# Where the two halves of each split weight unit lie in on-chip memory, and a 64-byte offset for the units of q, k and w_glu

## The chip, the cores and the metric

The kernel runs on one core of a Trainium2 chip. The time is device microseconds of one execution, taken as the median of several runs. One further execution was profiled; the views and the rows below come from it.

## What is computed

One decoder layer (depth 1) of width 2048 over 256 tokens. Three branches work side by side on the normalised input, their outputs are gated and summed, and a squared-ReLU MLP follows:

```python
proj = xn @ w_in          # 2048 x 11264: u_s5, u_lru, q, k, v, three gates
y_s5 = s5_branch(...)     # diagonal scan, gelu, y * sigmoid(y @ w_glu)
y_lru = rglru_branch(...)
y_attn = stick_breaking_attention(q, k, v)
merged = g_s5 * (y_s5 @ w_br_s5) + g_lru * (y_lru @ w_br_lru) + g_attn * (y_attn @ w_br_attn)
h = x + merged @ w_out
h = h + relu(rms_norm(h) @ w_up) ** 2 @ w_down
out = rms_norm(h)
```

Everything is float32. Nearly all of the time goes to the weight products.

## The kernel before

**Units.** All weight matrices are cut into units of 256 rows by 512 columns (two row blocks of 128, `UK = 2`, and `CH = 512` columns); a unit fills 128 partitions with 2 x 512 floats, 512 KB. The list `stream` fixes their order. Each unit is loaded by one DMA from the SP queue into a tile `raw` (three buffers), and split in two: ScalarE (ACT) writes the rounded copy `hi` (line 146), VectorE (DVE) writes the remainder `lo = raw - hi` (line 147). Both are float32r. The activations are split the same way (`xhi`, `xlo` and their like). A product is then three TensorE matmuls: high by high, high by low, low by high.

**Two forms of product.** In `chunk` (lines 225 to 227) the unit is the stationary operand, 128 columns at a time, and the activations are the moving one, 256 tokens wide: 2 row blocks x 4 column tiles x 3 = 24 matmuls a unit. It serves the columns 0 to 7 of `w_in`, 512 wide each (0 and 1: input of the S5 branch; 2 and 3: of the LRU branch; 4 and 5: q; 6 and 7: k), and `w_glu`. In `chunk_tok` (lines 241 to 243) and `pair_tok` (lines 276 to 278) the unit is the moving operand, 512 columns wide, and 128 tokens of the activations are stationary: 2 x 2 x 3 = 12 matmuls a unit. They serve all other products. Each matmul instruction has a weight load of its own, which the profile shows apart as PEld.

**Order.** `next_unit` keeps loads four units and splits three units ahead of the unit in use. The pools `whi` hold four buffers for `hi` and four for `lo`, so the split of a unit needs the matmuls of the unit four places earlier to be done. Side work (norms, the S5 scan, the LRU and the attention) is written as generators, which `pump` advances after every unit. Line 655 belongs to the S5 scan: it takes the sums `ps_y` from PSUM, whose matmuls are at line 653. `s5_stack` (line 631) copies pieces of `ux` into `stk` by DMAs on the SP queue, the queue of the unit loads (line 130). Tile addresses follow the order in which pools and tiles are made, in steps of 32 bytes; a scheduler orders the instructions of each engine.

**Addresses.** A byte address here is that within a partition, and its residue is that modulo 256. In the program before, `hi`, `lo`, `xhi`, `xlo` and all operands of the three forms of product begin at residue 32. The four `hi` buffers lie 4096 bytes apart, the four `lo` buffers too, and each stands off the activations by a multiple of 4096 bytes. Inside a tile the slices move by multiples of 512 bytes.

Of the kernel before, what the change touches and what calls it, by code (L numbers as in the profile page):

```python
# [9 lines left out]
F32 = mybir.dt.float32  # L10
F32R = mybir.dt.float32r
# [3 lines left out]
P = 128  # L15
# [3 lines left out]
CH = 512  # L19
UK = 2  # L20
W = 1024
WT = W // P
# [16 lines left out]
GELU_K = 0.044715  # L39


def units_of(k, n):
    return (n // CH) * (k // (P * UK))

# [2 lines left out]
def hybrid_block(ctx: ExitStack, tc: tile.TileContext, io, out):  # L47
# [2 lines left out]

    const = ctx.enter_context(tc.tile_pool(name="const", bufs=1))
    wraw = ctx.enter_context(tc.tile_pool(name="wraw", bufs=3))
    whi = ctx.enter_context(tc.tile_pool(name="whi", bufs=4))
    act = ctx.enter_context(tc.tile_pool(name="act", bufs=1))
    ypool = ctx.enter_context(tc.tile_pool(name="ypool", bufs=2))
    tmp = ctx.enter_context(tc.tile_pool(name="tmp", bufs=2))
    psm = ctx.enter_context(tc.tile_pool(name="psm", bufs=4, space=PSUM))
    pss = ctx.enter_context(tc.tile_pool(name="pss", bufs=4, space=PSUM))
# [2 lines left out]
    stream = []  # L61
# [36 lines left out]
    for q in range(NQ):  # L98
# [5 lines left out]
        for c in range(2, 4):  # L104
            stream.extend(("w_down", c, q * (FQ // (P * UK)) + g) for g in range(FQ // (P * UK)))
    ngrp = {"w_in": D, "w_br_lru": W, "w_br_attn": W, "w_br_s5": W, "w_glu": W,
            "w_out": D, "w_up": D, "w_down": DFF}

    raw, hi, anchor = {}, {}, {}
    st = {"load": 0, "split": 0, "use": 0}  # L110

    def pieces(i):
        return [slice(k, k + 1) for k in range(UK)] if i == 0 else [slice(0, UK)]
# [19 lines left out]
    def split_next():  # L133
        i = st["split"]
        if i >= len(stream):
            return
        st["split"] += 1
        h = whi.tile([P, UK, CH], F32R, tag="hi", name=f"hi{i}")
        l_ = whi.tile([P, UK, CH], F32R, tag="lo", name=f"lo{i}")
        r = raw.pop(i)  # L140
        x = anchor.pop("x", None)
        es = ExitStack()
        if i == 0:
            es.enter_context(tc.issue_after(x))
        for k in pieces(i):
            anchor["act"] = nc.scalar.copy(h[:, k, :], r[:, k, :]).ins  # L146
            anchor["dve"] = nc.vector.tensor_tensor(l_[:, k, :], r[:, k, :], h[:, k, :].bitcast(F32), ALU.subtract).ins  # L147
        es.close()
        hi[i] = h, l_

    def next_unit():
        i = st["use"]
        st["use"] += 1
        while st["load"] <= min(i + 4, len(stream) - 1):
            load_next()
            load_x(st["load"])
        while st["split"] <= min(i + 3, len(stream) - 1):
            before_split(st["split"])
            split_next()
        return (stream[i], *hi.pop(i))  # L160
# [126 lines left out]
    def small(name):  # L287
        o = 0
        for n_, w_ in PAR.items():
            if n_ == name:  # L290
                return par[:, o:o + w_]
            o += w_
# [39 lines left out]
    nc.gpsimd.affine_select(keep, ones, pattern=[[1, P]], compare_op=ALU.is_gt, fill=0.0, base=0, channel_multiplier=-1)  # L332
    drop = const.tile([P, P], F32, name="drop")
    nc.gpsimd.tensor_scalar(drop, keep, 1e30, -1e30, ALU.mult, ALU.add)
    eps_t = const.tile([P, 1], F32, name="eps_t")
    nc.gpsimd.memset(eps_t, EPS)
    half_pi = const.tile([P, 1], F32, name="half_pi")
    nc.gpsimd.memset(half_pi, math.pi / 2)
    magic = const.tile([P, 1], F32, name="magic")
    nc.gpsimd.memset(magic, MAGIC)  # L340

    def rsqrt_mean(o, ps, n):
# [4 lines left out]
        nc.vector.scalar_tensor_tensor(o, t, 1.5, r, ALU.add, ALU.mult)  # L347

    rstd = const.tile([P, L], F32, name="rstd")
    rstd_tok = const.tile([P, 2], F32, name="rstd_tok")  # L350

    def norm1():
        yield
# [131 lines left out]
    br_ = small("lru_b_r")  # L485
    bi_ = small("lru_b_i")
    lam = small("lru_lambda")
    sp4 = const.tile([P, WT], F32, name="sp4")
    nsp8 = const.tile([P, WT], F32, name="nsp8")
    tiny = const.tile([P, 1], F32, name="tiny")  # L490
    nc.gpsimd.memset(tiny, 2.0 ** -115)
    wrwi = sp.tile([P, 2, WT, P], F32, tag="stk", name="wrwi")
    wr, wi = wrwi[:, 0], wrwi[:, 1]
# [3 lines left out]
    def lru_load():  # L497
        for t, src in ((wr, "lru_w_r"), (wi, "lru_w_i")):
            for h in range(2):
                nc.sync.dma_start(t[h * 64:(h + 1) * 64, :, h * 64:(h + 1) * 64], io[src][h])  # L500
                yield

    def lru_params():
        for _ in range(4):
            yield
        lc = const.tile([P, 4, WT], F32, name="lc")
        nc.vector.scalar_tensor_tensor(lc[:, 0, :], lam, -1.0, lam, ALU.mult, ALU.min)
        nc.scalar.activation(lc[:, 1, :], lc[:, 0, :], AF.Exp)
        nc.scalar.activation(lc[:, 2, :], lc[:, 1, :], AF.Ln, bias=1.0)
        nc.vector.tensor_scalar(lc[:, 3, :], lam, -1.0, 0.0, ALU.mult, ALU.max)  # L510
        nc.vector.tensor_tensor(lc[:, 3, :], lc[:, 3, :], lc[:, 2, :], ALU.add)
        nc.vector.tensor_scalar(sp4, lc[:, 3, :], 4.0, None, ALU.mult)
        nc.vector.tensor_scalar(nsp8, lc[:, 3, :], -8.0, None, ALU.mult)
        yield
        yield from lru_load()
# [4 lines left out]
    def lru_half(c, us):  # L520
# [44 lines left out]
        for u, cts, xc, r, i_, th in parts:  # L565
# [5 lines left out]
            yield  # L571

    lq = later([lru_params()], 1.15)
    u_banks = {}

# [315 lines left out]
    for c in range(2):  # L891
        banks = chunk("w_glu", c, W, lambda kt: (yg_hi[:, kt, :], yg_lo[:, kt, :]))
        for j in range(2):
            g = tmp.tile([P, 2, L], F32, tag="gate", name=f"glu_{c}_{j}", bufs=3)
            for h in range(2):
                k = c * 4 + 2 * j + h
# [24 lines left out]
    for a in S5_TAIL:  # L921
        c = int(a[1])
# [52 lines left out]
                yield  # L975
        return gen

    rs2 = const.tile([P, 2], F32, name="rs2")
    rq, rfl = [deque(), 2.0, 0.0], {}

    def out_done(c, banks):
# [199 lines left out]
```

## Time and profile before

| | us |
|---|---|
| median of 3 runs | 1490.29 |
| lowest and highest | 1489.69, 1490.58 |
| the profiled execution, its own time | 1491.41 |
| its span in the trace | 1489.7 |
| TensorE busy in the span | 1478.5 |
| VectorE busy | 1175.7 |
| ScalarE busy | 775.4 |

The page gives for each engine its busy time, its share of the span and its instructions. A matmul's duration in the page is longer than the distance to the next one, since matmuls overlap: how fast TensorE gets on is read from the starts of matmuls that follow each other in the timeline, not from the durations. PEld rows are the weight loads of the same matmuls, which run beside the matmul before.

### The profile page before, as it was taken

The page shows a single profiled execution, that of the slowest core. Times are in us where ns is not written, and L with a number is a line of the kernel's source. Part 1 is how long each engine was busy: PE and PEld are TensorE (multiplying, and loading weights), DVE is VectorE, ACT ScalarE, POOL GpSimd, SP SyncE. Part 2 cuts the span into 40 slices and gives each one's busy share as a digit, 9 for nine tenths or more (in the row PEclk, how much of TensorE's full clock was granted, in tenths as well). Part 3 has the DMA queues.
Part 4 walks back from the last instruction along what each step waited for, and adds up shares of the span by engine and source line. Part 5 has one row for each costly group of instructions (what it writes and reads, how often), then busy time and mean ns, then how long its engine had stood idle before and what let it go on. Part 6 is the DMA issues. An engine that isn't in the chain of part 4 may idle for free.

```text
span 1489.7 us, 19903 instructions
## 1 busy us (share of the span) xinstructions
PE 1478.5 (99%) x7518; PEld 1259.3 (85%) x7518; DVE 1175.7 (79%) x1470; ACT 775.4 (52%) x915; POOL 48.4 (3%) x73
## 2 busy tenths in 40 slices
PE   9999999999999999999999999999999999999997
PEld 9998888989888888888888888888888888888886
DVE  6878999887989998789799896568754886458955
ACT  6767556565765564544454544344433453344443
POOL 1400000000000000000000000000000000000010
PEclk9999999999999999999999999999999999999999
DMA  9557776655556756566856657666666566666664
GB/s 274 189 157 216 209 229 208 184 165 188 170 177 199 224 184 210 188 187 210 268 183 189 195 184 222 189 193 188 200 194 196 187 197 197 192 190 196 189 198 137
DMA packets 89570, 292.41 MB, mean 196 GB/s; under 512 B 12802, under 2 KB 17026, under 8 KB 89346
## 3 DMA queue, kind: packets, MB, share of 16 engines
q1 hardware_dynamic: 89042, 290.55, 62.5%
q8 instruction: 59, 0.97, 0.3%
q10 hardware_dynamic: 432, 0.59, 0.1%
q14 instruction: 37, 0.30, 0.1%
HBM read 282.71 MB, written 2.10 MB: 191 GB/s over the span
## 4 chain that ended last, share of the span: by engine, by line
PE 95%; DVE 2%; ACT 1%; DMA 1%; issue 1%; DVEq 0%; ACTq 0%; SPq 0%
PE mt_w_in L241 7%; PE mt_w_in L243 7%; PE mt_w_in L242 7%; PE mt_w_up L241 7%; PE mt_w_up L243 7%; PE mt_w_up L242 7%; PE mp_w_down L278 4%; PE mp_w_down L277 4%; PE mp_w_down L276 4%; PE mt_w_down L242 4%; PE mt_w_down L241 4%; PE mt_w_down L243 4%; PE mm_w_in L225 3%; PE mm_w_in L227 3%; PE mm_w_in L226 3%; PE mt_w_br_attn L241 1%
## 5 line engine op out<-in xcount | busy, mean ns | idle before, releaser
L146 ACT CAST hi<-raw 128x1024 fp32r<-128x1024 f32 (+1 forms) x521 | 545.2, 1050 | 614.2 <-PE mt_w_up L243 116.8
L147 DVE TENSOR_TENSOR lo<-raw,hi 128x1024 fp32r<-128x1024 f32 (+1 forms) x521 | 637.1, 1224 | 276.2 <-ACT hi L146 268.5
L241 PE MATMUL mt_w_in<-hi,xhi 128*128 128x512 f32 x448 | 176.2, 393 | 0.0
L243 PE MATMUL mt_w_in<-hi,xlo 128*128 128x512 f32 x448 | 174.5, 389 | 0.0
L242 PE MATMUL mt_w_in<-lo,xhi 128*128 128x512 f32 x448 | 174.4, 389 | 0.0
L241 PE MATMUL mt_w_up<-hi,hhi 128*128 128x512 f32 x448 | 174.3, 389 | 0.0
L242 PE MATMUL mt_w_up<-lo,hhi 128*128 128x512 f32 x448 | 174.3, 389 | 0.0
L243 PE MATMUL mt_w_up<-hi,hlo 128*128 128x512 f32 x448 | 174.3, 389 | 0.0
L225 PE MATMUL mm_w_in<-xhi,hi 128*128 128x256 f32 x512 | 146.7, 287 | 0.7 <-ACT hi L146 0.7
L227 PE MATMUL mm_w_in<-xhi,lo 128*128 128x256 f32 x512 | 145.6, 285 | 1.4 <-DVE lo L147 1.4
L226 PE MATMUL mm_w_in<-xlo,hi 128*128 128x256 f32 x512 | 145.6, 285 | 0.0
L741 DVE STREAM_TRANSPOSE reluT<-relu 32x256 f32<-32x256 f32 x256 | 111.5, 436 | 4.2
L242 PE MATMUL mt_w_down<-lo,hd_hi 128*128 128x512 f32 (+1 forms) x272 | 102.5, 377 | 0.0
L241 PE MATMUL mt_w_down<-hi,hd_hi 128*128 128x512 f32 (+1 forms) x272 | 102.4, 377 | 0.0
L243 PE MATMUL mt_w_down<-hi,hd_lo 128*128 128x512 f32 (+1 forms) x272 | 102.4, 376 | 0.0
L225 PEld LDWEIGHTS mm_w_in<-xhi,hi 128*128 128x128 f32 x512 | 99.1, 194 | 1.9 <-ACT hi L146 1.0
L227 PEld LDWEIGHTS mm_w_in<-xhi,lo 128*128 128x128 f32 x512 | 98.8, 193 | 1.9 <-DVE lo L147 1.8
L276 PE MATMUL mp_w_down<-hi,hd_hi 128*128 128x512 f32 x256 | 99.6, 389 | 0.0
L277 PE MATMUL mp_w_down<-lo,hd_hi 128*128 128x512 f32 x256 | 99.6, 389 | 0.0
L278 PE MATMUL mp_w_down<-hi,hd_lo 128*128 128x512 f32 x256 | 99.6, 389 | 0.0
L226 PEld LDWEIGHTS mm_w_in<-xlo,hi 128*128 128x128 f32 x512 | 99.2, 194 | 0.1
L243 PEld LDWEIGHTS mt_w_in<-hi,xlo 128*128 128x128 f32 x448 | 84.1, 188 | 17.7
(294 smaller groups left out, 2358.1 us busy)
## 6 DMA issues: line engine op xcount, KB each, us to landing
raw<-in_w_in SPq DMA_DIRECT2D x175, 512.0 KB, 4.2
raw<-in_w_up SPq DMA_DIRECT2D x128, 512.0 KB, 4.3
raw<-in_w_down SPq DMA_DIRECT2D x128, 512.0 KB, 4.2
raw<-in_w_out SPq DMA_DIRECT2D x32, 512.0 KB, 4.4
raw<-in_w_br_lru SPq DMA_DIRECT2D x16, 512.0 KB, 4.6
raw<-in_w_br_attn SPq DMA_DIRECT2D x16, 512.0 KB, 4.3
raw<-in_w_br_s SPq DMA_DIRECT2D x16, 512.0 KB, 4.3
stk<-ux SPq DMA_DIRECT2D x96, 64.0 KB, 4.3
```

The source lines that it names most:

```text
L146: anchor["act"] = nc.scalar.copy(h[:, k, :], r[:, k, :]).ins
L147: anchor["dve"] = nc.vector.tensor_tensor(l_[:, k, :], r[:, k, :], h[:, k, :].bitcast(F32), ALU.subtract).ins
L225: nc.tensor.matmul(o, wh[:, kk, s], xh, start=first and ct % 2 == 0, stop=False, skip_group_check=True)
L226: nc.tensor.matmul(o, wh[:, kk, s], xl, start=False, stop=False, skip_group_check=True)
L227: mm = nc.tensor.matmul(o, wl[:, kk, s], xh, start=False, stop=last and ct % 2 == 1, skip_group_check=True)
L241: nc.tensor.matmul(banks[j], xh[:, s], wh[:, a:b], start=kt == 0, stop=False)
L242: nc.tensor.matmul(banks[j], xh[:, s], wl[:, a:b], start=False, stop=False)
L243: return nc.tensor.matmul(banks[j], xl[:, s], wh[:, a:b], start=False, stop=kt == ng * UK - 1)
L276: nc.tensor.matmul(o, xh[:, s], wh[:, kk, :], start=kt == 0, stop=False)
L277: nc.tensor.matmul(o, xh[:, s], wl[:, kk, :], start=False, stop=False)
L278: mm = nc.tensor.matmul(o, xl[:, s], wh[:, kk, :], start=False, stop=kt == ng * UK - 1)
L741: nc.vector.transpose(d_[32 * a:32 * a + 32, :, :, 32 * b:32 * b + 32], s_[32 * b:32 * b + 32, :, :, 32 * a:32 * a + 32])
```

## The change

The pool `whi` goes. A new pool `wsplit` holds four slots with tags `w0` to `w3`, one for every fourth unit. A slot holds the high half, behind it the low half, and 16 floats (64 bytes) to spare. The function `shift` says where in the slot a unit begins: at the slot's start, or 16 floats (64 bytes) on for `w_glu` and for columns 4 to 7 of `w_in`. A slot takes 8256 bytes. Small tiles that lay in the pool `const` are put between the slots, with some filling (`row`), so that slots stand 8448 bytes apart, 33 times 256.

```diff
+SLOTS = 4
+SHIFT = 16
+
+
+def shift(name, c, g):
+    return SHIFT if name == "w_glu" or name == "w_in" and 4 <= c < 8 else 0
...
-    whi = ctx.enter_context(tc.tile_pool(name="whi", bufs=4))
     act = ctx.enter_context(tc.tile_pool(name="act", bufs=1))
     ypool = ctx.enter_context(tc.tile_pool(name="ypool", bufs=2))
+    wsplit = ctx.enter_context(tc.tile_pool(name="wsplit", bufs=1))
...
+    def slot(i):
+        return wsplit.tile([P, 2 * UK * CH + SHIFT], F32R, tag=f"w{i % SLOTS}", name=f"w{i % SLOTS}_{i}")
+
+    def row(name, n, used=None):
+        return wsplit.tile([P, n], F32, name=name)[:, 0:used or n]
+
+    first = [slot(0)]
+    lc, sp4, nsp8 = row("lc", 4 * WT).rearrange("p (a k) -> p a k", a=4), row("sp4", WT), row("nsp8", WT)
+    first.append(slot(1))
+    eps_t, half_pi, magic, tiny = (row(n, 1) for n in ("eps_t", "half_pi", "magic", "tiny"))
+    rstd_tok = row("rstd_tok", 16, 2)
+    first.append(slot(2))
+    rs2 = row("rs2", 48, 2)
+    first.append(slot(3))
...
-        h = whi.tile([P, UK, CH], F32R, tag="hi", name=f"hi{i}")
-        l_ = whi.tile([P, UK, CH], F32R, tag="lo", name=f"lo{i}")
+        o = shift(*stream[i])
+        w = (first[i] if i < SLOTS else slot(i))[:, o:o + 2 * UK * CH]
+        h, l_ = (w[:, a:a + UK * CH].rearrange("p (k c) -> p k c", k=UK) for a in (0, UK * CH))
```

The other lines of the diff take the tiles `eps_t`, `half_pi`, `magic`, `tiny`, `rstd_tok`, `sp4`, `nsp8`, `lc` and `rs2` out of the pool `const`.

In the program after, every operand of the three forms of product begins at residue 160, except the shifted units: their `hi` and `lo` begin at residue 224, 64 bytes on from the activations that they meet. Slots 0 and 2 stand off the activations by a multiple of 512 bytes, slots 1 and 3 by 256 bytes more.

TensorE has the same matmuls in the same order, with the same engines waited for. This is the start of the first q unit on TensorE, before, where `hi` and `lo` are two tiles:

```order
1588 L227 MATMUL mm_w_in_1_80_2536<-xhi,lo_2690 128x256
1589 L225 MATMUL mm_w_in_0_88_2825<-xhi,hi_2720 128x256 [waits Activation_49]
1590 L226 MATMUL mm_w_in_0_88_2825<-xlo,hi_2720 128x256
1591 L227 MATMUL mm_w_in_0_88_2825<-xhi,lo_2721 128x256 [waits DVE_49]
1592 L225 MATMUL mm_w_in_0_88_2825<-xhi,hi_2720 128x256
```

And the same place on TensorE after the change, where `w_88` is the slot of unit 88:

```order
1588 L251 MATMUL mm_w_in_1_80_2454<-xhi,w_87_2603 128x256
1589 L249 MATMUL mm_w_in_0_88_2735<-xhi,w_88_2633 128x256 [waits Activation_49]
1590 L250 MATMUL mm_w_in_0_88_2735<-xlo,w_88_2633 128x256
1591 L251 MATMUL mm_w_in_0_88_2735<-xhi,w_88_2633 128x256 [waits DVE_49]
1592 L249 MATMUL mm_w_in_0_88_2735<-xhi,w_88_2633 128x256
```

Nothing moved: the first high matmul waits for ScalarE alone, and the first low one for VectorE.

On VectorE the subtraction of a unit no longer waits for TensorE. Within the first k columns VectorE has, before, this order; `lo_2591` is the low half of unit 84:

```order
249 L147 TENSOR_TENSOR lo_2540<-raw_2500,hi_2539 128x1024 [waits DMAHW6_49,Activation_49]
250 L621 TENSOR_TENSOR ux<-us_99,ux 128x256 [waits Activation_49]
251 L625 SCALAR_TENSOR_TENSOR ux<-bco,par,ux 128x2x64 [waits Activation_49] x2
252 L147 TENSOR_TENSOR lo_2591<-raw_2537,hi_2590 128x1024 [waits DVE_49,DMAHW7_49,PE_49,Activation_49]
253 L655 SCALAR_TENSOR_TENSOR us_99<-us_99,par,ps_y_2578 128x256 [waits PE_49]
254 L679 TENSOR_TENSOR s_t<-s_v,tc_2110 128x1024 [waits DVE_49]
```

The same place on VectorE after the change:

```order
247 L171 TENSOR_TENSOR w_83_2457<-raw_2419,w_83_2457 128x1024 [waits DMAHW6_49,Activation_49]
248 L637 TENSOR_TENSOR ux<-us_112,ux 128x256 [waits Activation_49]
249 L641 SCALAR_TENSOR_TENSOR ux<-bco,par,ux 128x2x64 [waits Activation_49] x2
250 L671 SCALAR_TENSOR_TENSOR us_112<-us_112,par,ps_y_2495 128x256 [waits PE_49]
251 L171 TENSOR_TENSOR w_84_2507<-raw_2455,w_84_2507 128x1024 [waits DMAHW7_49,DVE_49,Activation_49]
252 L695 TENSOR_TENSOR s_t<-s_v,tc_2046 128x1024 [waits DVE_49]
```

The subtraction of unit 84 moved behind the instruction that takes `ps_y` out of PSUM (line 655 before, 671 after), which waits for TensorE. The same swap is made once more, at unit 122. The wait of a subtraction on TensorE went, since ScalarE, which writes the slot first, holds that wait for both halves. In a `chunk` unit ScalarE now waits for the last matmul of the unit four places earlier, where it waited for the last but one.

On the SP queue three unit loads change places with one small DMA of `s5_stack` each. Before, at the second such place:

```order
160 L631 DMA stk<-ux 32x512 [waits DMAHW1_49]
161 L130 DMA raw_2827<-in_w_in 128x1024 [waits DMAHW2_49,DVE_49]
162 L631 DMA stk<-ux 32x2x256 [waits DMAHW3_49]
163 L130 DMA raw_2861<-in_w_in 128x1024 [waits DMAHW5_49,DMAHW4_49,DVE_49]
```

The same place on the SP queue after the change:

```order
160 L647 DMA stk<-ux 32x512 [waits DMAHW1_49]
161 L647 DMA stk<-ux 32x2x256 [waits DMAHW2_49]
162 L153 DMA raw_2737<-in_w_in 128x1024 [waits DMAHW3_49,DVE_49]
163 L153 DMA raw_2770<-in_w_in 128x1024 [waits DMAHW5_49,DMAHW4_49,DVE_49]
```

One unit load moved one place back. On ScalarE and VectorE a few instructions of one LRU step change places too.

More of the change, by code (lines that the diff above doesn't have):

```diff
@@ L334, in hybrid_block @@
     nc.gpsimd.tensor_scalar(drop, keep, 1e30, -1e30, ALU.mult, ALU.add)
-    eps_t = const.tile([P, 1], F32, name="eps_t")
     nc.gpsimd.memset(eps_t, EPS)
-    half_pi = const.tile([P, 1], F32, name="half_pi")
     nc.gpsimd.memset(half_pi, math.pi / 2)
-    magic = const.tile([P, 1], F32, name="magic")
     nc.gpsimd.memset(magic, MAGIC)
@@ L349, in hybrid_block @@
     rstd = const.tile([P, L], F32, name="rstd")
-    rstd_tok = const.tile([P, 2], F32, name="rstd_tok")
     def norm1():
@@ L487, in hybrid_block @@
     lam = small("lru_lambda")
-    sp4 = const.tile([P, WT], F32, name="sp4")
-    nsp8 = const.tile([P, WT], F32, name="nsp8")
-    tiny = const.tile([P, 1], F32, name="tiny")
     nc.gpsimd.memset(tiny, 2.0 ** -115)
@@ L505, in lru_params @@
             yield
-        lc = const.tile([P, 4, WT], F32, name="lc")
         nc.vector.scalar_tensor_tensor(lc[:, 0, :], lam, -1.0, lam, ALU.mult, ALU.min)
@@ L976, in residual @@
         return gen
-    rs2 = const.tile([P, 2], F32, name="rs2")
     rq, rfl = [deque(), 2.0, 0.0], {}
```

## The prediction

> **What bounds the kernel now.** I read the page's shares first, then who waited for whom on TensorE, then the timeline of TensorE, because the page's matmul durations overlap and say nothing of the pace.
>
> ```profile
> span 1489.7 us, 19903 instructions
> PE 1478.5 (99%) x7518; PEld 1259.3 (85%) x7518; DVE 1175.7 (79%) x1470; ACT 775.4 (52%) x915; POOL 48.4 (3%) x73
> ...
> PEclk9999999999999999999999999999999999999999
> ...
> PE 95%; DVE 2%; ACT 1%; DMA 1%; issue 1%; DVEq 0%; ACTq 0%; SPq 0%
> ```
>
> TensorE is busy 99% of the span at the full granted clock, and 95% of the chain that ended last is its own. The waits on TensorE confirm it; these three rows are all there are:
>
> ```profile
> PE mm_w_in L227 <- DVE lo L147: 1.4, 1, 1.4
> PE warm L327 <- POOL eps_t L336: 1.0, 1, 1.0
> PE mm_w_in L225 <- ACT hi L146: 0.7, 1, 0.7
> ```
>
> So 3.1 us of waits in the whole span. Nothing that feeds TensorE can gain more than a few us; only the pace of the matmuls themselves can. That pace is in the starts. The next rows are the timeline of TensorE: first and second matmul of the first q columns, their last and the one after; then the same of four columns of `w_up`.
>
> ```profile
> 269.47 0.28 PE L225 MATMUL mm_w_in<-xhi,hi 128*128 128x256 f32 x1
> 269.59 0.28 PE L226 MATMUL mm_w_in<-xlo,hi 128*128 128x256 f32 x1
> ...
> 292.39 0.28 PE L227 MATMUL mm_w_in<-xhi,lo 128*128 128x256 f32 x1
> 292.51 0.40 PE L241 MATMUL mt_w_in<-hi,xhi 128*128 128x512 f32 x1
> ...
> 958.54 0.39 PE L241 MATMUL mt_w_up<-hi,hhi 128*128 128x512 f32 x1
> 958.77 0.39 PE L242 MATMUL mt_w_up<-lo,hhi 128*128 128x512 f32 x1
> ...
> 1045.36 0.39 PE L243 MATMUL mt_w_up<-hi,hlo 128*128 128x512 f32 x1
> 1045.59 0.39 PE L276 MATMUL mp_w_down<-hi,hd_hi 128*128 128x512 f32 x1
> ```
>
> The q columns are 8 units of 24 matmuls, 192 in (292.51 - 269.47) = 23.04 us: 120.0 ns each, without a gap. The `w_up` columns are 32 units of 12, 384 in 87.05 us: 226.7 ns each. The step from 256 to 512 columns costs 106.7 ns, so each float32r matmul pays 13.3 ns that do not depend on its width. Plain float32 passes of the attention pay less:
>
> ```profile
> 310.41 0.60 PE L819 MATMUL ps_c<-s,tri 128*128 128x256 f32 x2
> 310.84 0.38 PE L820 MATMUL ps_c<-s,ones 128*128 128x128 f32 x2
> 311.06 0.39 PE L821 MATMUL ps_c<-s,tri 128*128 128x128 f32 x2
> 311.28 0.60 PE L806 MATMUL ps_z<-qT,kT 128*128 128x256 f32 x2
> ```
>
> Six passes over 2 x 256 + 4 x 128 = 1024 columns take 0.87 us. Two passes of 256 take 0.43 us and two of 128 take 0.22 us, so 128 columns cost about 0.105 us, half the float32r rate; at 106.7 ns for 128 columns the passes need 0.853 us and 2.8 ns remain for each. A float32r matmul therefore pays 10.5 ns beyond what a weight change needs. Both kinds load 128 columns of weights for each matmul, and both read weights and moving data at one residue. What differs is the moving operand's speed: it runs at the weight read's speed in float32 and at twice that in float32r. That fits two reads of the same memory that overtake each other, but it fits a fixed cost of float32r as well; no row of this trace tells them apart.
>
> **The change, part by part.**
>
> *The offset of 64 bytes.* It touches four column blocks of `w_in` (two of q, two of k) of 8 x 24 matmuls and two of `w_glu` of 4 x 24: 768 + 192 = 960 matmuls, 115.2 us of the span at 120.0 ns. All other matmuls of the three forms keep equal residues. No matmul of the trace has unequal ones, so the cost is bounded. These are weight loads, mean duration behind the bar after the busy time:
>
> ```profile
> L226 PEld LDWEIGHTS mm_w_glu<-yg_lo,hi 128*128 128x128 f32 x64 | 12.3, 192 | 0.0
> ...
> L242 PEld LDWEIGHTS mt_w_up<-lo,hhi 128*128 128x128 f32 x448 | 84.1, 188 | 17.4
> ```
>
> The same load of 128 columns takes 192 ns beside a 256-wide stream and 188 ns beside a 512-wide one. In the 256-wide form the load is on the path: the timeline above leaves 120.0 ns from one matmul to the next, and the load that must end between them fills all of it (PEld idle 0.0 in the first row, 17.4 us in the second). I read the 4 ns as the least that the meeting of the two reads costs here. Lower bound of the time: the whole excess goes, 960 x 10.5 ns = 10.1 us gained. Upper bound: a further meeting. During one load of 512 bytes the moving read passes 1024 bytes, so it overtakes the weight read by 512 bytes, twice round a circle of 256. If the excess is those meetings, each costs 10.5 / 2 = 5.25 ns. The offset of 64 bytes is a quarter of the circle and moves every meeting by an eighth of the load, some 13 ns; one can fall out of the load at its end, or one more can fall in, which costs 960 x 5.25 ns = 5.0 us. I take the value nearest to a row, the 4 ns: **960 x 4 ns = 3.8 us gained**.
>
> *The order of TensorE* is the same and so is what it waits for, so nothing is added there.
>
> *Equal residues elsewhere, 32 before and 160 now.* The two operands move together, so I take nothing. The one relative change is that slots 1 and 3 stand 256 bytes off a multiple of 512 now. That matters only if the memory repeats at 512 bytes rather than at 256; the trace can't tell, since all offsets of before are multiples of 512. Units of the 512-wide form number 448 of 520, with 12 matmuls each; half of those 5376, 2688, would then change by up to 5.25 ns, 14 us either way. I take zero, the row of 226.7 ns being the same for all offsets that do occur (0, 512, 1024 and more).
>
> *One tile for both halves.* ScalarE waits one matmul longer for a slot in the 256-wide form, 0.12 us. What hides it is the lead of three units, shown by the splits in the middle of the first k columns:
>
> ```profile
> 263.79 1.05 ACT L146 CAST hi<-raw 128x1024 fp32r<-128x1024 f32 x1 [1.78 <-PE mm_w_in L226]
> 266.67 1.05 ACT L146 CAST hi<-raw 128x1024 fp32r<-128x1024 f32 x1 [1.83 <-PE mm_w_in L226]
> ...
> DVE lo L147 <- PE ps_y L653: 1.8, 1, 1.8
> DVE lo L147 <- PE mt_w_br_lru L243: 1.7, 1, 1.7
> ```
>
> ScalarE splits one unit every 2.88 us, is busy 1.05 us of it and idle 1.83 us; a split begins when the unit four places earlier is done, and TensorE has three more units, 8.6 us, before it needs the result. 0.12 us is nothing against that. The last two rows show all that the subtractions waited for TensorE: 3.5 us in two waits, neither of which TensorE felt. Their end gains nothing.
>
> *The swaps.* The subtraction of unit 84 is now queued behind an instruction that waits for TensorE's `ps_y`. Those matmuls and VectorE's work after them:
>
> ```profile
> 248.22 1.07 PE L653 MATMUL ps_y<-s_t,ce 128*32 128x256 f32 x16
> ...
> 250.83 1.23 DVE L147 TENSOR_TENSOR lo<-raw,hi 128x1024 fp32r<-128x1024 f32 x1 [0.75 <-ACT hi L146]
> 251.97 0.48 DVE L655 SCALAR_TENSOR_TENSOR us<-us,par,ps_y 128x256 f32<-128x256 f32 x1
> ```
>
> `ps_y` is done at 249.3, before VectorE comes to either, so the subtraction moves by at most 0.48 us, inside the 0.75 us that it waited anyway or the 8.6 us of lead. Queued behind it on VectorE is S5 work with no reader on TensorE in that unit. The three unit loads on the SP queue move behind one small copy each. A load is issued four units ahead, lands within about 4 us by the next row, and the q stretch has room; without that cover each would cost at most the copy's own 4 us:
>
> ```profile
> raw<-in_w_in SPq DMA_DIRECT2D x175, 512.0 KB, 4.2
> stk<-ux SPq DMA_DIRECT2D x96, 64.0 KB, 4.3
> ...
> 269.40:292.30 22.90, 22.90 (x193) 22.90 (x193) 17.64 (x20) 13.57 (x13) 0.00 (x0) 1.00 0.55 176
> ```
>
> The last row is the first q columns, 22.9 us: TensorE and its loads full, VectorE 17.64 us, ScalarE 13.57 us, DMA engines at a share of 0.55. If TensorE runs 3% faster there, VectorE at 77% still keeps up. So nothing becomes late next.
>
> Sum: the profiled execution's own time, 1491.41 us, less 3.8 us is 1487.6 us. The median of the runs shown lies 1.1 us below that execution, at 1490.29, so I forecast **1486.5 us**.
>
> A rule of the Trainium skill speaks against any effect. Its page "SBUF — State Buffer", section "Who interferes with whom", gives TensorE two independent read ports, one for moving data and one for weight loads, and says "PE and ACT never wait on anyone." By it the sum would be zero and the time 1490.3 us; the 192 against 188 ns of the same load are the row that does not fit it. Its page "TensorE: Matmul & The Clock Gate", section "Back-to-back issue gap", gives N / 2.4 + 2.5 ns, an estimate of 109 and 216 ns for 256 and 512 columns; the trace has 120.0 and 226.7, and if the offset brought the 256-wide form to that estimate, 960 matmuls would save 10.6 us.
>
> **The rivals.**
>
> *Nothing happens.* The 13.3 ns are a fixed cost of switching weights in float32r. For it speaks that the excess is the same to 0.1 ns at both widths and at all offsets in the trace; against it the float32 passes and the 192 ns. Time: 1490.3 us.
>
> *Slower, by one more meeting.* The offset brings a third meeting into each load instead of taking one out: 960 x 5.25 ns = 5.0 us, in the q, k and `w_glu` stretches alone. It decides as soon as the distance there passes 123 ns (3 us over 960 matmuls). For it speaks that equal starts may be the best phase: in float32 both reads start together, stay together, and pay 2.8 ns. Time: 1495.3 us.
>
> *The slots at 256 bytes.* If 512 bytes is the period, the 512-wide matmuls of every second unit change by up to 5.25 ns, 14 us up or down: 1476 or 1504 us. Only the sameness at multiples of 512 speaks of it, and that on neither side.
>
> **How the numbers follow.** Forecast (some of the excess goes, about 4 ns, at most 10.5 ns): 0.46. Nothing: 0.35. One more meeting: 0.15. The slots: 0.04, half to each side. A measurement of this kernel can tell about 0.2%, 3 us, from no change. Of the forecast's 0.46 about 0.05 lies below 3 us and counts as no change, as does 0.01 of the slower rival. So faster 0.41 + 0.02 = 0.43, same 0.35 + 0.06 = 0.41, slower 0.14 + 0.02 = 0.16. The range goes from all of the excess (1490.3 - 10.1 = 1480.2) to the one more meeting (1495.3): 1480 to 1495.5, which leaves out the slots and little else that I can price, with some room for prices that I can't. The likeliest case's own range is 1480 to 1489.
>
> **What would show it right or wrong.** In the timeline of TensorE the starts in q, k and `w_glu` stand about 116 ns apart instead of 120.0, the weight loads of `mm_w_glu` take 188 ns instead of 192, and the first four column blocks keep 120.0. With 120.0 throughout, the offset does nothing; with 123 or more, the slower rival holds. The `w_up` rows must stay at 226.7 ns; if units alternate there, it is the slots. New waits of TensorE for `lo`, `hi` or a DMA would show the moved instructions wrong. The prediction is wrong altogether if the gain or loss lies in the 512-wide matmuls.

## The result, and the profile after

| | before | after |
|---|---|---|
| median of 6 runs, us | 1490.43 | 1484.99 |
| lowest and highest, us | 1489.69, 1491.01 | 1484.10, 1487.49 |
| the profiled execution, its own time, us | 1491.41 | 1485.22 |
| its span, us | 1489.7 | 1483.5 |

The ratio is 0.9966, with a 95% interval of 0.9954 to 0.9978: 5.4 us faster in the medians, 1.5 us below the forecast of 1486.5. The span fell by 6.2 us.

The page after, its span, shares and the chain that ended last:

```profile
span 1483.5 us, 19900 instructions
PE 1471.6 (99%) x7518; PEld 1251.8 (84%) x7518; DVE 1175.8 (79%) x1470; ACT 774.8 (52%) x915; POOL 48.6 (3%) x73
...
PE 93%; DVE 2%; DMA 2%; ACT 1%; issue 1%; POOL 0%; SPq 0%; DVEq 0%; ACTq 0%
```

TensorE is still busy 99% of the span, with as many matmuls as before, but 6.9 us less of it; no other engine's busy time moved by more than 0.6 us. All waits of TensorE after (total, times, longest):

```profile
PE mm_w_in L251 <- DVE w L171: 2.3, 2, 1.8
PE warm L351 <- POOL eps_t L359: 1.0, 1, 1.0
PE mm_w_in L249 <- ACT w L170: 0.4, 1, 0.4
```

3.7 us, against 3.1 before: the gain isn't a wait that went. It is in the starts. The timeline of TensorE after, at the places shown of before: the first q columns from their first matmul to the one behind their last, then the two columns of `w_glu` from the first matmul of each to the one behind, then four columns of `w_up`:

```profile
268.06 0.28 PE L249 MATMUL mm_w_in<-xhi,w 128*128 128x256 f32 x1
268.18 0.28 PE L250 MATMUL mm_w_in<-xlo,w 128*128 128x256 f32 x1
...
289.82 0.40 PE L265 MATMUL mt_w_in<-w,xhi 128*128 128x512 f32 x1
...
581.79 0.38 PE L249 MATMUL mm_w_glu<-yg_hi,w 128*128 128x256 f32 x1
...
592.78 0.28 PE L249 MATMUL mm_w_glu<-yg_hi,w 128*128 128x256 f32 x1
...
603.66 0.40 PE L265 MATMUL mt_w_br_s<-w,ys_hi 128*128 128x512 f32 x1
...
952.35 0.39 PE L265 MATMUL mt_w_up<-w,hhi 128*128 128x512 f32 x1
...
1039.39 0.39 PE L300 MATMUL mp_w_down<-w,hd_hi 128*128 128x512 f32 x1
```

The 192 q matmuls take 289.82 - 268.06 = 21.76 us, **113.33 ns** from start to start, where it was 120.0. The second column of `w_glu` takes 603.66 - 592.78 = 10.88 us for 96, again 113.3 ns. The 384 matmuls of `w_up` take 87.04 us, 226.7 ns, as before. Summed over the matmuls of a block, for each from its start to the start of TensorE's next matmul:

| matmuls | before, us | after, us | difference |
|---|---|---|---|
| k and q columns, 4 x 192 | 92.57 | 87.90 | -4.67 |
| `w_glu`, 2 x 96 | 23.14 | 21.87 | -1.27 |
| first four columns of `w_in`, 4 x 192 | 96.87 | 96.68 | -0.19 |

The shifted blocks give 5.95 us. At a full 6.67 ns each, 960 matmuls would give 6.4 us. Of the missing 0.45 us some 0.3 us are three of the 40 shifted units, the first of the first k column and two of the last q column, which run at a steady 117.8 ns instead of 113.3; the experiments below meet this second pace again.

The weight loads, with the mean duration behind the busy time:

```profile
L250 PEld LDWEIGHTS mm_w_glu<-yg_lo,w 128*128 128x128 f32 x64 | 12.0, 188 | 0.0
...
L266 PEld LDWEIGHTS mt_w_up<-w,hhi 128*128 128x128 f32 x448 | 84.1, 188 | 17.4
```

Those of `w_glu` went from 192 to 188 ns and those of `w_up` stayed. The faster TensorE is fed: in the first q columns the two engines that split the units have room. The row gives the stretch, its length, and the busy time of TensorE, its loads, VectorE, ScalarE and GpSimd, then the granted clock, the DMA share and GB/s:

```profile
268.00:289.70 21.70, 21.70 (x193) 21.70 (x193) 18.19 (x21) 13.60 (x13) 0.98 (x1) 1.00 0.67 197
```

VectorE is busy 84% of it and ScalarE 63%, and TensorE has no gap.

### The profile page after: what moved, and what is told of

Read it like the earlier page. It is cut to its first block, busy times and chain, and to the rows that moved or that the text cites. A ratio compares the mean times of both kernels' runs of the same rounds, so it can differ in the third digit from the quotient of the medians.

```text
span 1483.5 us, 19900 instructions
## 1 busy us (share of the span) xinstructions
PE 1471.6 (99%) x7518; PEld 1251.8 (84%) x7518; DVE 1175.8 (79%) x1470; ACT 774.8 (52%) x915; POOL 48.6 (3%) x73
## 4 chain that ended last, share of the span: by engine, by line
PE 93%; DVE 2%; DMA 2%; ACT 1%; issue 1%; POOL 0%; SPq 0%; DVEq 0%; ACTq 0%
PE mt_w_in L265 7%; PE mt_w_in L266 7%; PE mt_w_in L267 7%; PE mt_w_up L266 7%; PE mt_w_up L265 7%; PE mt_w_up L267 7%; PE mp_w_down L300 4%; PE mp_w_down L302 4%; PE mp_w_down L301 4%; PE mt_w_down L266 4%; PE mt_w_down L265 4%; PE mt_w_down L267 4%; PE mm_w_in L249 2%; PE mm_w_in L251 2%; PE mm_w_in L250 2%; DMA raw<-in_w_in 2%
## 5 line engine op out<-in xcount | busy, mean ns | idle before, releaser
L170 ACT CAST w<-raw 128x1024 fp32r<-128x1024 f32 (+1 forms) x521 | 545.6, 1050 | 612.9 <-PE mt_w_up L267 129.6
L171 DVE TENSOR_TENSOR w<-raw,w 128x1024 fp32r<-128x1024 f32 (+1 forms) x521 | 636.9, 1224 | 268.4 <-ACT w L170 264.0
L265 PE MATMUL mt_w_in<-w,xhi 128*128 128x512 f32 x448 | 176.3, 394 | 0.0
L266 PE MATMUL mt_w_in<-w,xhi 128*128 128x512 f32 x448 | 174.6, 390 | 0.0
L267 PE MATMUL mt_w_in<-w,xlo 128*128 128x512 f32 x448 | 174.5, 390 | 0.0
L265 PE MATMUL mt_w_up<-w,hhi 128*128 128x512 f32 x448 | 174.3, 389 | 0.0
L266 PE MATMUL mt_w_up<-w,hhi 128*128 128x512 f32 x448 | 174.3, 389 | 0.0
L267 PE MATMUL mt_w_up<-w,hlo 128*128 128x512 f32 x448 | 174.3, 389 | 0.0
L251 PE MATMUL mm_w_in<-xhi,w 128*128 128x256 f32 x512 | 143.4, 281 | 2.3 <-DVE w L171 2.3
L249 PE MATMUL mm_w_in<-xhi,w 128*128 128x256 f32 x512 | 144.1, 282 | 0.5 <-ACT w L170 0.4
L250 PE MATMUL mm_w_in<-xlo,w 128*128 128x256 f32 x512 | 143.1, 280 | 0.0
L266 PE MATMUL mt_w_down<-w,hd_hi 128*128 128x512 f32 (+1 forms) x272 | 102.5, 377 | 0.0
L265 PE MATMUL mt_w_down<-w,hd_hi 128*128 128x512 f32 (+1 forms) x272 | 102.4, 377 | 0.0
L300 PE MATMUL mp_w_down<-w,hd_hi 128*128 128x512 f32 x256 | 99.6, 389 | 0.0
L301 PE MATMUL mp_w_down<-w,hd_hi 128*128 128x512 f32 x256 | 99.6, 389 | 0.0
```

The costliest lines, as they stand in the source:

```text
L249: nc.tensor.matmul(o, wh[:, kk, s], xh, start=first and ct % 2 == 0, stop=False, skip_group_check=True)
L250: nc.tensor.matmul(o, wh[:, kk, s], xl, start=False, stop=False, skip_group_check=True)
L251: mm = nc.tensor.matmul(o, wl[:, kk, s], xh, start=False, stop=last and ct % 2 == 1, skip_group_check=True)
L265: nc.tensor.matmul(banks[j], xh[:, s], wh[:, a:b], start=kt == 0, stop=False)
L266: nc.tensor.matmul(banks[j], xh[:, s], wl[:, a:b], start=False, stop=False)
L267: return nc.tensor.matmul(banks[j], xl[:, s], wh[:, a:b], start=False, stop=kt == ng * UK - 1)
```

## The experiments

In what follows an offset is the byte address of the weight load's operand less that of the moving operand, modulo 256. For a unit that is the stationary operand it is the shift itself; for one that is the moving operand it is 256 less the shift.

### The packing without the offset

```diff
 def shift(name, c, g):
-    return SHIFT if name == "w_glu" or name == "w_in" and 4 <= c < 8 else 0
+    return 0
```

> All of the change but the 64 bytes: units of q, k and w_glu begin at their slot's start. Theory A (the offset between the two operands sets the pace): q, k and w_glu go back from 113.3 to 120.0 ns between starts, the time goes back to that of before, 1490.4 us, within 1 us. Theory B (the shared tile does it, by fewer waits and another order): the time stays at 1485 us and the starts at 113.3 ns.

Measured: 1490.51 us against 1490.28, ratio 1.0002 with an interval of 0.9993 to 1.0011. The timeline of the first q columns in this run, and then a group of the loads of `w_glu`:

```profile
268.36 0.28 PE L249 MATMUL mm_w_in<-xhi,w 128*128 128x256 f32 x1
...
291.40 0.40 PE L265 MATMUL mt_w_in<-w,xhi 128*128 128x512 f32 x1
```

```profile
L250 PEld LDWEIGHTS mm_w_glu<-yg_lo,w 128*128 128x128 f32 x64 | 12.3, 192 | 0.0
```

23.04 us again, 120.0 ns each, and loads of 192 ns. This kernel has the shared tile, the swaps on VectorE and SP, all residues at 160 and slots at 256 bytes from each other; they are worth nothing together, to within 0.1%. The whole gain is the 64 bytes. With equal residues the distance is 120.0 ns at residue 32 (before) and at 160 (here), which speaks for the relative place of the two operands. In the first sweep below, units that begin at residue 32 as before, but 128 bytes from their activations, stand 118.7 ns apart; so the unit's own residue doesn't set the distance alone. A pair 64 bytes apart at other residues than 224 and 160 was not tried for this form.

### The offset for all 256-wide products

```diff
-    return SHIFT if name == "w_glu" or name == "w_in" and 4 <= c < 8 else 0
+    return SHIFT if name == "w_glu" or name == "w_in" and c < 8 else 0
```

> The offset also for the units of the first four column blocks (w_in columns 0 to 3), 768 matmuls more. Theory A: they go from 120.0 to 113.3 ns, 768 x 6.67 = 5.1 us less than after, 1479.9 us. Rival C (the first stage is paced by loads and splits, not by TensorE): the starts are nearer but TensorE waits more, and the time stays within 2 us of 1485.

Measured: 1486.0 us, ratio 0.9962 with an interval of 0.9948 to 0.9976. The changed kernel had a ratio of 0.9966 with 0.9954 to 0.9978. So four more columns brought nothing that can be told. In the profile of this run (its execution took 1488.46 us, the longest of the five) 22 of the 32 units of these columns do run at 113.3 ns, 6 at 117.8, and 4 are broken by a stop or by other matmuls. Yet the four columns together take 97.8 us, against 96.7 and 96.1 in two profiles of the changed kernel: the time went into gaps. The last of these columns in this run, the matmuls ahead of and behind the longest gap and two a little later, with what ended the gap in brackets; then two windows of this run over that stretch, and the longer one of the changed kernel:

```profile
90.09 0.28 PE L250 MATMUL mm_w_in<-xlo,w 128*128 128x256 f32 x1
92.66 0.38 PE L251 MATMUL mm_w_in<-xhi,w 128*128 128x256 f32 x1 [2.29 <-DVE w L171]
...
94.38 0.42 PE L249 MATMUL mm_w_in<-xhi,w 128*128 128x256 f32 x1
94.60 0.41 PE L250 MATMUL mm_w_in<-xlo,w 128*128 128x256 f32 x1
```

```profile
92.70:96.20 3.50, 3.50 (x22) 3.50 (x23) 3.50 (x7) 0.00 (x0) 0.00 (x0) 0.70 0.63 174
...
82.00:110.00 28.00, 24.72 (x184) 23.75 (x183) 19.68 (x30) 20.32 (x33) 0.00 (x0) 0.94 0.50 153
```

```profile
82.00:110.00 28.00, 26.22 (x205) 25.59 (x204) 19.54 (x30) 20.14 (x33) 0.00 (x0) 1.00 0.49 151
```

The first two rows are a stop of 2.57 us for VectorE's half of a unit. The same stop was 1.71 us before, and 2.06 and 1.09 us in the two profiles of the changed kernel. That the units of this stage don't come faster than they are used, so that a quicker TensorE only waits longer, fits these rows; since the stop differs by 1 us between two profiles of one kernel, it is not shown by its length alone. Behind the stop the matmuls stand some 214 ns apart for a while and the granted clock of the stretch is 0.70; in the changed kernel it is 1.00 throughout. So in this execution the stage also lost time to a slower clock.

The gaps are not all. The k and q columns have the same addresses here as in the changed kernel, and take 89.16 us against 87.90. From the second k column on, 13 units in a row run at 117.8 ns, at the full clock and with no wait of TensorE inside them. Shown are the first matmul of the second unit of that column and the first of the column behind it, then the stretch between them, then the column's weight loads, those of the low half first:

```profile
327.54 0.28 PE L249 MATMUL mm_w_in<-xhi,w 128*128 128x256 f32 x1
...
347.33 0.28 PE L249 MATMUL mm_w_in<-xhi,w 128*128 128x256 f32 x1
```

```profile
327.50:347.30 19.80, 19.80 (x170) 19.80 (x170) 14.22 (x17) 8.40 (x8) 0.55 (x2) 1.00 0.51 160
```

```profile
L251 PEld LDWEIGHTS mm_w_in<-xhi,w 128*128 128x128 f32 x63 | 12.1, 192 | 0.0
L250 PEld LDWEIGHTS mm_w_in<-xlo,w 128*128 128x128 f32 x63 | 11.8, 188 | 0.0
L249 PEld LDWEIGHTS mm_w_in<-xhi,w 128*128 128x128 f32 x63 | 11.8, 188 | 0.0
```

168 matmuls in 19.79 us are 117.8 ns each. In both profiles of the changed kernel this column runs at 113.3 ns. So at an offset of 64 bytes the pace is 113.3 or 117.8 ns, and stays at either for many units; the offset alone does not say which. At equal residues the steady pace of this form is 120.0 ns in every profile. What chooses between the two was not found.

### The offset for the first column of the S5 branch as well

```diff
-    return SHIFT if name == "w_glu" or name == "w_in" and 4 <= c < 8 else 0
+    return SHIFT if name == "w_glu" or name == "w_in" and (c == 0 or 4 <= c < 8) else 0
```

> The offset also for column block 0 of w_in, the one of the first four that came out shorter with the offset in all four (22.2 against 23.4 us). Theory A alone: 192 x 6.67 = 1.3 us less than after, 1483.7 us. Rival C (the first stage is paced by what feeds TensorE): column 0 gets 1.2 us shorter and column 1 behind it longer by about as much, the total within 1 us of after.

Measured: 1486.86 us, ratio 0.9977 with an interval of 0.9968 to 0.9987; the changed kernel on the same chip is the next run below. Against its profile column 0 fell from 23.39 to 22.19 us, and the next column rose from 24.47 to 26.07: the 1.2 us are given back within the next 26 us. The next column alone is weak evidence, since it took 25.45 us in the other profile of the changed kernel, but the medians say the same: 1486.86 us here, 1486.07 without this column's offset. No version of the offset was found that beats the changed kernel.

The changed kernel once more, as it is:

> The changed kernel unaltered, timed beside the next one on the same chip. All theories: 0.9964 of before, 1485 us.

Measured: 1486.07 us, ratio 0.997 with an interval of 0.9958 to 0.9982. The gain came again on this chip, 4.3 us in the medians.

### Only the low half shifted

```diff
-        w = (first[i] if i < SLOTS else slot(i))[:, o:o + 2 * UK * CH]
-        h, l_ = (w[:, a:a + UK * CH].rearrange("p (k c) -> p k c", k=UK) for a in (0, UK * CH))
+        w = first[i] if i < SLOTS else slot(i)
+        h, l_ = (w[:, a:a + UK * CH].rearrange("p (k c) -> p k c", k=UK) for a in (0, UK * CH + o))
```

> In q, k and w_glu the low half alone lies 64 bytes on, the high half at the slot's start: of three weight loads one has the offset of 64 and two that of 0. If each load's own offset sets the distance before its matmul: 113.3 ns once in three and 120.0 twice, a mean of 117.8 and a third of the gain, 2.1 us. If the steady state needs all loads at the offset: 120 throughout, no gain; if one load in three is enough, 113.3 throughout.

Measured: 1487.82 us in one execution. The first q columns in this run:

```profile
267.47 0.28 PE L249 MATMUL mm_w_in<-xhi,w 128*128 128x256 f32 x1
...
290.09 0.39 PE L265 MATMUL mt_w_in<-w,xhi 128*128 128x512 f32 x1
```

22.61 us for 192, 117.8 ns each: three matmuls take 353.3 ns, which is 113.3 + 2 x 120.0. One load in three is offset, and a third of the gain comes (2.0 us over all shifted blocks, of 5.95). The forecast mean is met, but not the picture behind it: no distance in this column is 113 or 120 ns, all lie between 117 and 119. The loads of `w_glu` in this run, line 250 for the high half and 251 for the low one:

```profile
L251 PEld LDWEIGHTS mm_w_glu<-yg_hi,w 128*128 128x128 f32 x64 | 12.3, 192 | 0.0
L250 PEld LDWEIGHTS mm_w_glu<-yg_lo,w 128*128 128x128 f32 x64 | 12.0, 188 | 0.0
```

The offset half has the 192 ns, and the high half, which was not moved, 188. This is, to the nanosecond, the second pace of the run with all halves shifted: 117.8 ns, with loads of 192, 188 and 188 ns. Since that pace also comes with all three loads offset, this run does not show that each load counts by its own offset. It shows that with the low half alone no unit of the shifted columns reached 113.3 ns.

### Other offsets

Three kernels give each block an offset of its own, and `w_up` too, where the unit is the moving operand. In the first:

```diff
 def shift(name, c, g):
-    return SHIFT if name == "w_glu" or name == "w_in" and 4 <= c < 8 else 0
+    if name == "w_in":
+        return {2: 44, 3: 24, 0: 32, 1: 40, 6: 48, 4: 8, 7: 4, 5: 12}.get(c, 0)
+    if name == "w_glu":
+        return (20, 0)[c]
+    if name == "w_up" and c >= 4:
+        return (0, 8, 16, 24, 32, 40, 48, 44, 4, 12, 20, 28)[c - 4]
+    return 0
```

The slots have room for 48 floats in these three, and the small tiles between them lie elsewhere.

> Another offset for each block of columns, one look. Stationary operand ahead of the moving one, in bytes modulo 256: 256-wide form 0, 16, 32, 48, 80, 96, 128, 160, 176, 192; 512-wide form (w_up, columns 4 to 15) 0, 64, 80, 96, 128, 144, 160, 176, 192, 208, 224, 240. Theory A (two reads that overtake each other): the distance of starts depends on the offset in both forms, some offsets give 8 cycles of 1.2 GHz less (113.3 and 220.0 ns) and some perhaps more than 120.0 and 226.7. Theory D (the offset only eases the weight load, which is on the path in the 256-wide form alone): the 512-wide form stays at 226.7 ns at every offset. Theory E (a fixed cost of 13.3 ns, with 64 bytes a special case): all but few offsets give 120.0.

The second asks for steps of 4 bytes around 64, 0 and 88:

```diff
+    if name == "w_in":
+        return {6: 14, 4: 15, 7: 17, 5: 18}.get(c, 0)
+    if name == "w_glu":
+        return (16, 22)[c]
+    if name == "w_up" and c >= 4:
+        return (1, 2, 3, 5, 6, 7, 9, 10, 11, 14, 18, 22)[c - 4]
```

> A finer sweep, one look. Stationary ahead of moving in bytes modulo 256: 256-wide form 56, 60, 64, 68, 72, 88; 512-wide form 252, 248, 244, 236, 232, 228, 220, 216, 212, 200, 184, 168; the first four column blocks at 0. Theory A with two reads that overtake each other: the pace changes by steps as a meeting leaves the load, so there is a range around 64 with 113.3 ns and a range just below 256 with 226.7. Rival F (only the exact offsets 64 and 0 fit, as lines of the memory): one step of 4 bytes off and the pace is 117 ns or more, and 229 or more.

The third changes the offset from unit to unit, 24 matmuls at each in the 256-wide form and 24 in the 512-wide one:

```diff
+    if name == "w_in" and 4 <= c < 8:
+        u = (6, 4, 7, 5).index(c) * 8 + g
+        return 2 * u if u < 25 else (16, 22, 26, 30, 34, 38, 42)[u - 25]
+    if name == "w_up" and c >= 4:
+        return ((c - 4) * 8 + g) // 2
```

> Another offset for each unit, one look: the 256-wide form in steps of 8 bytes from 0 to 192, the 512-wide form (low to high in w_up, two units each) in steps of 4 bytes from 256 down to 68. If 64 and 88 are two of several good offsets of the 256-wide form, other units show 113.3 ns in their steady part too, and one of them perhaps less; if they are the edges of a range, all from 64 to 88 show it but 80, which had 119.8. The 512-wide form: no offset under 226.7 ns if 0 is its best.

The three took 1495.25, 1496.11 and 1498.12 us in one execution each, all slower than before. From the second, the second column of `w_glu` at offset 88, then the columns 7 and 9 of `w_up` at 236 and 228, each from its first matmul to the one behind its last:

```profile
595.90 0.28 PE L257 MATMUL mm_w_glu<-yg_hi,w 128*128 128x256 f32 x1
...
606.78 0.40 PE L273 MATMUL mt_w_br_s<-w,ys_hi 128*128 128x512 f32 x1
...
1022.77 0.40 PE L273 MATMUL mt_w_up<-w,hhi 128*128 128x512 f32 x1
...
1045.80 0.40 PE L308 MATMUL mp_w_down<-w,hd_hi 128*128 128x512 f32 x1
...
1155.29 0.40 PE L273 MATMUL mt_w_up<-w,hhi 128*128 128x512 f32 x1
...
1177.11 0.40 PE L273 MATMUL mt_w_up<-w,hhi 128*128 128x512 f32 x1
```

96 matmuls each: 10.88 us is 113.3 ns, 23.03 us is 239.9 ns, 21.82 us is 227.3 ns. From the third, the first matmuls of successive units at offsets 64, 72, 80, 88 and 96:

```profile
269.65 0.29 PE L256 MATMUL mm_w_in<-xhi,w 128*128 128x256 f32 x1
...
272.39 0.28 PE L256 MATMUL mm_w_in<-xhi,w 128*128 128x256 f32 x1
...
275.24 0.28 PE L256 MATMUL mm_w_in<-xhi,w 128*128 128x256 f32 x1
...
278.08 0.28 PE L256 MATMUL mm_w_in<-xhi,w 128*128 128x256 f32 x1
...
280.81 0.28 PE L256 MATMUL mm_w_in<-xhi,w 128*128 128x256 f32 x1
```

The units at 64 and 88 take 2.74 and 2.73 us, those at 72 and 80 take 2.85 and 2.84. The distances of the 256-wide form from the three runs are means over the last two thirds of each unit's matmuls, single stops left out; a block is a whole column of `w_in` or `w_glu`, and a single unit comes from the third run:

| offset, bytes | 256-wide, block, ns | single units, ns |
|---|---|---|
| 0 | 120.0 | 120.0 |
| 8 | - | 115.8 |
| 16 | 120.0 | 118.4 |
| 32 | 118.3 | 118.4 |
| 48 | 117.8 | 118.6 |
| 56 | 118.2 | 118.0 |
| 60 | 119.5 | - |
| **64** | **113.3** | **113.4**, **113.4** |
| 68 | 118.4 | - |
| 72 | 118.3 | 118.4 |
| 80 | 118.7 | 118.7 |
| **88** | **113.3** | **113.4**, **113.6** |
| 96 | 117.5 | 117.6 |
| 128 | 118.7 | 118.6 |
| 168 | - | **113.6**, 119.9 |
| 192 | 117.8 | 117.6 |

Those of the 512-wide form are means over a block, or over the last two thirds of the 24 matmuls:

| offset, bytes | 512-wide, ns |
|---|---|
| **0** | **226.7** |
| 252, 248, 244, 240, 236 | 237.8, 234.3, 228.9, 231.7, 239.9 |
| 232, 228, 224, 220, 216 | 233.5, 227.3, 233.4, 234.7, 233.3 |
| 196, 192, 148, 128 | 227.3, 229.0, 227.1, 233.2 |
| 156, 124, 100, 64 | 239.9, 240.0, 228.0, 233.2 |

The other offsets tried lie between these, but for a single unit of the 256-wide form at 24 bytes, with 121.4 ns. Some offsets show more than one pace here too: 168 has 113.6 and 119.9 ns, 16 has 120.0 and 118.4, and 152 (not listed) 117.7 and 120.0. A single unit or block is therefore no proof of what an offset can do at its best. Three things follow. First, no range of offsets with the full gain was found: 4 bytes to either side of 64 a whole column stood at 119.5 and 118.4 ns, and neither has a unit at 113.3. Second, the 512-wide form depends on the offset as well, and the equal residues that it has are the best that were found; 49 offsets in steps of 4 bytes gave none below 226.7 ns. Third, 226.7 is twice 113.33, and 240.0 is twice 120.0. Each 256 columns of either form take from 113.3 to some 121 ns; at offset 0 the 512-wide form stands at its best and the 256-wide one near its worst. Of the theories put down ahead, the one in which the offset only eases the load of the 256-wide form fell, since the 512-wide form moves too, and so did the ranges of good offsets that two overtaking reads would give; the exact places held at 64, but 88 is good as well.

## Why the prediction was right, and where it was not

**TensorE's pace sets the time: right.** 5.95 us of the span's 6.2 us are shorter distances of shifted matmuls, while its waits rose by 0.6 us.

**The term of 960 x 4 ns was mis-sized.** The text read the difference of two loads, 192 and 188 ns, as "the least that the meeting of the two reads costs here" and took 3.8 us. Measured were 6.67 ns for each matmul in most units and 5.95 us in all. The loads did fall to 188 ns, as forecast, but their 4 ns are not the size of the gain: at 120.0 ns all three loads of a group last 192 ns, at 117.8 one of them, at 113.3 none, so 4 ns of load stood for 6.67 ns of distance. The distance was to be 116 ns and is 113.3.

**The split of the distance into 106.7 ns and a fixed 13.3 ns fell.** It compared two widths at one offset and took the same excess at both for a cost that does not depend on the width. The sweeps show that at this offset one form is at its best and the other near its worst; at the best of each, 113.3 and 226.7 ns, nothing is left that does not grow with the width. And the lower bound, all of the 10.5 ns gone, was not to be had by any offset tried: by the prediction's own split the best leaves 6.67 of the 13.3 ns, one half. The picture of two equal meetings of which one falls out gives just this half, 6.67 ns, if the whole excess is divided; the prediction divided the 10.5 ns instead and had 5.25. The picture has no support beyond that number: by it a change of 4 bytes should do next to nothing, and at 60 and 68 bytes most of the gain was gone; nor has it a place for two paces at one offset.

**The rule of the Trainium skill fell with it.** The page "SBUF — State Buffer", section "Who interferes with whom", gives TensorE two independent read ports and says "PE and ACT never wait on anyone." Here the same matmuls with the same loads stand 113.3 or 120.0 ns apart, and 226.7 or 240.0 ns, when nothing but the place of their operands is changed. The measurement decides: where the operands lie is not free for TensorE. That it is the two reads that hold each other up fits this, and no run shows it.

**The edits costed at nothing: right.** The packing, the swaps and the slots at 256 bytes gave a ratio of 1.0002 together. The slots rival fell: the `w_up` matmuls keep 226.7 ns in all slots. So did the rival of nothing: with the offset alone taken back, the distance is 120.0 ns again.

**The rival of one more meeting** is not what this offset does to this form. In the other form it would have been slower: `w_up` at the same relative 64 bytes has 233.2 ns instead of 226.7, and 240.0 at worst.

**Left open.** That the 64 bytes bring the gain is shown by taking them back; why is not. Why 64 and 88 bytes do it and 60, 68, 72 and 80 didn't, why 0 is best at 512 columns and bad at 256, and why a unit at 64 bytes sometimes runs at 117.8 ns, was not found. The first four columns of `w_in` stayed at 120.0 ns as forecast; whether they could gain with more lead of loads and splits was not tried.

## What to carry to other kernels

Where TensorE changes its weights with every matmul and is the bound, the relative address of weights and moving data is worth a sweep in steps of 4 bytes, for each width apart, with several units at each offset since one offset can have two paces: what helped one form by 5.6% would have cost the other 3%. Take the offset only where TensorE isn't waiting for its operands; in a stage that is fed too slowly the time turns into gaps. And read the size of such a cost from the distance of starts, not from the duration of a load.

## What the runs showed that was not expected

- The distance of matmuls changes with an offset of 4 bytes: 119.5, 113.3 and 118.4 ns at 60, 64 and 68 bytes, in one run.
- At 64 bytes there are two steady paces, 113.3 and 117.8 ns, with the same addresses, the full clock and no waits; 13 units in a row took the slower one in one profile, where two profiles of the changed kernel ran the same 13 at the faster.
- The 512-wide form goes from 226.7 to 240.0 ns by the offset, 6%, and keeps its best value in this kernel, where its residues are equal.
- Two stops of TensorE of 1.27 and 2.57 us, 3 us apart, were followed by a stretch at a granted clock of 0.70, with starts some 214 ns apart; a single stop at the same place of 2.06 us, in the changed kernel, was not, nor one of 2.44 us, in the run with one more column. Which of the stops' length and number decides was not tried apart.
